# Differential-attention scores: each half on 64 rows of the matmul array, three paired 64-row products, instead of two 128-row products per half

## The chip, the core and the metric

The kernel runs on one core of a Trainium2 chip. The metric is the device time of one execution in microseconds. TensorE (PE in the profile, with its weight loads as PEld) does the matrix products, VectorE (DVE), ScalarE (ACT) and GpSimd (POOL) the elementwise work, and SyncE (SP) issues nearly all DMA transfers.

## The reference

One step of a hybrid attention layer: a normalised input (2048 prompt tokens and 64 sample tokens, 1024 wide) goes through one input projection. Its columns feed eight "fox" heads of forgetting attention (64 wide, causal, with a bias from cumulated log-forget gates) and four heads of differential attention. Outputs are gated, concatenated, projected, normalised and added to the input. The part that the change touches is the differential attention:

```python
def diff_attention(q1, q2, k1, k2, v, lam, rel_bias, q_pos, k_pos):
    ...
        def probs(qi, ki):
            s = jnp.einsum('bqhd,bkhd->bhqk', qi, ki).astype(jnp.float32) * scale + bias
            return jax.nn.softmax(jnp.where(mask, s, NEG_INF), axis=-1)

        p = probs(q1i, k1) - lam * probs(q2i, k2)
        return jnp.einsum('bhqk,bkhd->bqhd', p.astype(v.dtype), v)
```

A differential head has two halves, (q1, k1) and (q2, k2), each 64 wide, that share the values and the bias. The prompt has 2048 queries and keys; the sample has 64 queries on 512 cached and 64 new keys.

## The kernel before

**Precision.** Every float32 operand is split into two float32r parts, h (the rounded value) and l (the rest), and a product is made as h·h + h·l + l·h in float32r.

**Work.** The tokens are cut into four blocks of 512. A unit is two fox heads (units 0 to 3) or one differential head (units 4 to 7). The projection of block b+1 runs beside the attention of block b (class `Proj`, `Attn`), and the output projection beside the last block's attention (class `Out`). Within attention a sub-job is one unit (or one fox head) and one pair of 128-query tiles. Its scores (stage A) run beside the products with the values (stage B) of the sub-job before. The order of the differential units: they come last in blocks 0 and 2, and first in blocks 1 and 3 (line 1424), so that there are two long stretches of differential work.

**Scores before.** `scores()` (L317 to L380) handles one query tile of one half. A head's operand tiles hold 128 rows: 64 rows of the h part and 64 rows of the l part. There are two query tiles for each half, (h|l) and (l|h), and one key tile (h|l). The first product gives h·h + l·l and the second l·h + h·l, so that a chunk of keys (128 to 512 wide, one PSUM bank) costs two products of 128 rows:

```python
                    S = ps.tile([P, BLK], F32, name="S", tag="S", bufs=3)
                    for s in (0, 1):
                        nc.tensor.matmul(S[:rows, :c1 - c0], q()[s][:, qc:qc + rows], kg()[ki][:, c0 - k0:c1 - k0],
                                         start=(s == 0), stop=(s == 1))
```

DVE then adds the bias to each chunk and keeps a running minimum (L359), and ACT takes the exponential (L372). `diff()` (L558) calls `scores()` once for each half and query tile (L578 to L581), then combines both halves (L583). Fox heads use the same `scores()`.

**The values.** `products()` (L463) transposes the probabilities on PE into a PSUM bank named pt (L490), splits them with ACT (L496) and DVE (L497), and multiplies them with the values (L521: av for fox, avd for differential heads).

**PSUM.** There are eight banks: three with the tag S, three with the tag pt, one av and one acc. The projection of the first two blocks borrows S banks (`acc()`, L785).

**What sets the order.** Python lists the work on a line of places (`put`, `merge`), and the tile framework's scheduler then orders the instructions of every engine from its own estimate of their durations. The products of one accumulation may therefore stand apart from one another in PE's stream, with other work between them. PE executes its stream in that order.

**Loads.** Keys and queries pass through DRAM. `k_out()` (L951) stores keys to KS with two DMAs, one for each half; `qgroup()` (L1018) does so for the queries to QD. `want_k()` (L189) loads key tiles into a ring of four slots. `want_q()` (L260) loads the two query tiles of a half with three DMAs into a ring of six slots (L267, L270). `want_kc()` (L200) makes the sample's keys from the cache.

## Time and profile before

| what | us |
|---|---|
| three timed runs | 1841.33, 1835.74, 1825.93 |
| their median | 1835.74 |
| span of the profiled execution, first to last instruction | 1837.8 |
| PE busy in it | 1736.8 |
| DVE busy | 1189.6 |
| ACT busy | 1128.9 |
| POOL busy | 768.2 |

The profiled execution is known by its span; what lies outside its first and last instruction is not shown, and the span stands 2.1 us above the median of the timed runs. A PE matmul row is named by rows*columns of the stationary operand, so that 128*64 means 128 rows and 64 columns of the array in use, and by the moving operand: 128x512 is 128 rows of 512 columns. The duration of a matmul covers its way through the array, and the next matmul begins before it ends; how long PE is held by one is read from the distance of two starts. "x2" merges neighbouring rows of one line.

### The profile page before, as it was taken

To read this page: it belongs to the slowest core of one execution; us is meant where nothing else is said; L and a number is where in the kernel's file an instruction comes from. 1 tells how busy PE (TensorE), PEld (TensorE's weight loads), DVE (VectorE), ACT (ScalarE), POOL (GpSimd) and SP (SyncE) were. 2 spreads that over 40 slices of the span, in tenths; PEclk is the share of its full clock that TensorE was granted. 3 is DMA by queue.
4 is the path that set the end of the run, shared out by engine and by line. 5 is a ranking of instruction groups with operands and counts; after the bars stand their busy time and mean duration, and the time that the engine had idled before them with its cause. 6 is when DMAs were issued, how large, how long until landed. Compare 5 with 4: busy or idle time off the path is not lost. (4 is left out here: it accounts for less than half of the span.)

```text
span 1837.8 us, 31858 instructions
## 1 busy us (share of the span) xinstructions
PE 1736.8 (95%) x9828; PEld 1467.4 (80%) x9828; DVE 1189.6 (65%) x3274; ACT 1128.9 (61%) x2518; POOL 768.2 (42%) x1083
## 2 busy tenths in 40 slices
PE   7888999999999999989999999999989999999998
PEld 5676888777877778878888888888878878887887
DVE  5422555556668576656776678878867876666764
ACT  4533656465767666665666657667776666556663
POOL 2204235345354453343323225555795663322331
PEclk9998999999999999999999999999989999999999
DMA  7787579789868766867777667667665464455433
GB/s 203 240 193 193 162 217 273 205 245 233 218 209 246 213 196 195 233 170 230 219 229 224 177 181 216 195 195 224 199 219 166 145 189 156 153 181 156 145 115 108
DMA packets 308170, 361.38 MB, mean 197 GB/s; under 512 B 41808, under 2 KB 202732, under 8 KB 308000
## 3 DMA queue, kind: packets, MB, share of 16 engines
q1 hardware_dynamic: 306384, 356.93, 66.9%
q0 software_dynamic: 672, 2.38, 0.4%
q8 instruction: 79, 1.29, 0.3%
q14 instruction: 91, 0.75, 0.1%
q10 hardware_dynamic: 944, 0.03, 0.0%
HBM read 263.89 MB, written 97.70 MB: 197 GB/s over the span
## 5 line engine op out<-in xcount | busy, mean ns | idle before, releaser
L372 ACT ACTIVATE prob<-prob,mn 128x1024 f32<-128x1024 f32 (+8 forms) x400 | 356.1, 892 | 180.7 <-DVE mn L359 179.5
L351 PE MATMUL S<-kg,qg 128*128 128x512 f32 (+4 forms) x1344 | 375.8, 373 | 20.5 <-DVE mn L359 10.0
L497 DVE TENSOR_TENSOR ptl<-pt,pth 128x512 fp32r<-128x512 f32 (+3 forms) x456 | 284.4, 636 | 94.8 <-ACT pth L496 92.3
L868 PE MATMUL acc<-wh,xx 128*128 128x512 f32 x752 | 303.4, 408 | 18.9 <-ACT wh L776 14.9
L869 PE MATMUL acc<-wl,xx 128*128 128x512 f32 x752 | 300.6, 401 | 8.5 <-DVE wl L777 8.5
L870 PE MATMUL acc<-wh,xx 128*128 128x512 f32 x752 | 300.6, 400 | 0.1
L496 ACT CAST pth<-pt 128x512 fp32r<-128x512 f32 (+3 forms) x456 | 237.6, 545 | 81.9 <-PE pt L490 65.4
L351 PEld LDWEIGHTS S<-kg,qg 128*128 128x128 f32 (+1 forms) x1344 | 226.6, 188 | 62.0 <-DVE mn L359 18.8
L490 PE MATMUL pt<-ident,prob 128*128 128x128 f32 (+2 forms) x1692 | 257.6, 274 | 4.7 <-ACT pts L637 2.2
L490 PEld LDWEIGHTS pt<-ident,prob 128*128 128x128 f32 (+2 forms) x1692 | 200.2, 142 | 26.6 <-ACT pts L637 3.3
L777 POOL TENSOR_TENSOR wl<-wraw,wh 128x512 fp32r<-128x512 f32 x126 | 167.4, 1345 | 121.2 <-ACT wh L776 91.0
L408 POOL TENSOR_TENSOR dg<-bias,cmask 128x128 f32<-128x128 f32 (+1 forms) x136 | 66.1, 486 | 281.8 <-DVE mn L359 188.4
L868 PEld LDWEIGHTS acc<-wh,xx 128*128 128x128 f32 x752 | 144.2, 193 | 49.7 <-ACT wh L776 17.2
L869 PEld LDWEIGHTS acc<-wl,xx 128*128 128x128 f32 x752 | 144.6, 192 | 37.3 <-DVE wl L777 11.5
L521 PE MATMUL av<-pth,vg 128*128 128x256 f32 (+1 forms) x576 | 158.3, 294 | 9.4 <-DVE oT L537 4.7
L870 PEld LDWEIGHTS acc<-wh,xx 128*128 128x128 f32 x752 | 144.0, 191 | 28.4 <-DVE xx L745 0.6
L521 PE MATMUL av<-ptl,vg 128*64 128x256 f32 (+1 forms) x576 | 140.3, 283 | 3.9 <-DVE ptl L497 3.6
L776 ACT CAST wh<-wraw 128x512 fp32r<-128x512 f32 x168 | 100.5, 618 | 69.1 <-DMA wraw<-in_w_in 59.9
L359 DVE CUSTOM_DVE_ANT_0 prob<-S,bias,mn 128x512 f32<-128x512 f32 (+4 forms) x200 | 115.3, 577 | 28.8 <-DMA bias<-CUM 14.5
L521 PE MATMUL avd<-pth,vg 128*128 128x256 f32 (+1 forms) x576 | 131.6, 288 | 2.3 <-ACT pth L496 2.3
L521 PEld LDWEIGHTS av<-pth,vg 128*128 128x128 f32 x576 | 110.0, 191 | 21.5 <-issue 7.7
L453 POOL TENSOR_SCALAR gate<-gate,rr 128x64 f32<-128x64 f32 (+1 forms) x136 | 61.5, 463 | 140.2 <-DMA gate<-GS 57.9
(257 smaller groups left out, 3611.8 us busy)
## 6 DMA issues: line engine op xcount, KB each, us to landing
wraw<-in_w_in SPq DMA_DIRECT2D x168, 256.0 KB, 4.8
vg<-VS SPq DMA_DIRECT2D x80, 512.0 KB, 4.1
kg<-KS SPq DMA_DIRECT2D x160, 256.0 KB, 4.1
bias<-CUM SPq DMA_DIRECT2D x80, 256.0 KB, 5.6
wst<-in_w_in SPq DMA_DIRECT2D x64, 256.0 KB, 5.6
out<-ef SPq DMA_DIRECT2D x64, 256.0 KB, 3.3
VS<-vhl SPq DMA_DIRECT2D x32, 512.0 KB, 4.6
KS<-khl SPq DMA_DIRECT2D x64, 256.0 KB, 4.7
```

The source lines that it names most:

```text
L351: nc.tensor.matmul(S[:rows, :c1 - c0], q()[s][:, qc:qc + rows], kg()[ki][:, c0 - k0:c1 - k0], start=(s == 0), stop=(s == 1))
L359: nc.vector.tensor_tensor_reduce(out=pr[:rows, a - p0:b - p0], in0=S[:rows, a - c0:b - c0], in1=ap()[:rows, a - b0:b - b0], scale=1.0, sca ...
L372: nc.scalar.activation(out=pr, in_=pr, func=AF.Exp, scale=-1.0, bias=st["m"][:rows, i - 1:i], accum_out=st["s"][:rows, h:h + 1])
L490: nc.tensor.transpose(pt[:rk, off:off + rows], self.key_tile(sts[j], rows, kt, rk), ident[:rows, :rows])
L496: nc.scalar.copy(h[:rk, :off], pt[:rk, :off])
L497: nc.vector.tensor_tensor(out=l[:rk, :off], in0=pt[:rk, :off], in1=r32(h[:rk, :off]), op=ALU.subtract)
L521: nc.tensor.matmul(st["av"][:vs.stop - vs.start, j0 * rows:W], ctxu["v"][kt // 4][:rk, kt % 4, vs], g["p"][part][:rk, o:o + w], start=(kt ...
L776: nc.scalar.copy(h, raw[:, :BLK])
L777: (nc.vector if many or k % 4 == 3 else nc.gpsimd).tensor_tensor(out=l, in0=raw[:, :BLK], in1=r32(h), op=ALU.subtract)
L868: nc.tensor.matmul(a, x[0][:, c0:c0 + rows], wh, start=s, stop=False)
L869: nc.tensor.matmul(a, x[0][:, c0:c0 + rows], wl, start=False, stop=False)
L870: nc.tensor.matmul(a, x[1][:, c0:c0 + rows], wh, start=False, stop=e)
```

## The change

`diff()` now calls a new function, `scores2()`, once for each query tile, for both halves. The operand tiles are laid out anew: one tile holds the h part and one the l part, and in each, rows 0 to 63 belong to the first half and rows 64 to 127 to the second. A chunk of keys takes two S banks, one for each half, and six products of 64 rows: h·h, h·l and l·h, written for the first half on rows 0 to 63 and for the second on rows 64 to 127 in turn. Fox heads keep `scores()`. There are four S banks and two pt banks (three and three before). Stores, loads and the sample's cached keys follow the layout; queries take two loads for a pair of query tiles and both halves (six before), and both halves' key tiles are asked for together. Comments are removed as well, so that line numbers differ.

```diff
+        def want_k2(self, got, u, nk):
+            def load(s, k0, k1):
+                def go():
+                    t = self.p["k"].tile([P, 2 * BLK], F32R, name="kg", tag="k")
+                    for c in range(k0, k1, BLK):
+                        nc.sync.dma_start(out=r32(t[:, c - k0:c - k0 + BLK]), in_=KS[c // BLK][s, u])
+                    got[s].append(t)
+                return go
+            for e in self.key_edges(nk):
+                for s in (0, 1):
+                    self.want(self.K, load(s, *e))
...
-                if s == 0:
+                    if u >= 4:
+                        nc.sync.dma_start(out=r32(t[:, :w]), in_=src[s, u, :, c0:c0 + w])
+                    elif s == 0:
...
-                    S = ps.tile([P, BLK], F32, name="S", tag="S", bufs=3)
+                    S = ps.tile([P, BLK], F32, name="S", tag="S", bufs=4)
...
+        def scores2(self, q, qc, rows, kg, n, bias, sts, last, nk):
...
+            for ki, k0, c0, c1, end in cuts:
+                def chunk(ki=ki, k0=k0, c0=c0, c1=c1, end=end):
+                    S = [ps.tile([P, BLK], F32, name="S", tag="S", bufs=4) for _ in (0, 1)]
+                    for a, b in ((0, 0), (0, 1), (1, 0)):
+                        for i in (0, 1):
+                            r = slice(64 * i, 64 * i + 64)
+                            nc.tensor.matmul(S[i][:rows, :c1 - c0], q()[a][r, qc:qc + rows],
+                                             kg()[b][ki][r, c0 - k0:c1 - k0], start=(a + b == 0), stop=(a == 1))
+                    for half, st in enumerate(sts):
+                        for b0, b1, ap in bias:
...
+                    if last and end:
+                        self.K.free()
+                        self.K.free()
+                th.append(((c1 - c0) * 3 / 2400.0, chunk))
...
-                    pt = ps.tile([P, BLK], F32, name="pt", tag="pt", bufs=3)
+                    pt = ps.tile([P, BLK], F32, name="pt", tag="pt", bufs=2)
...
-                for i in (0, 1):
-                    q = ctxu["q"][(pair, i)]
-                    A += self.scores(lambda q=q: q, j * rows, rows, lambda i=i: ctxu["k"][i], n, pieces, sts[j][i],
-                                     last and j == len(tiles) - 1, ctxu["nk"], i)
+                A += self.scores2(lambda: ctxu["q"][(pair, 0)], j * rows, rows, lambda: ctxu["k"], n, pieces, sts[j],
+                                  last and j == len(tiles) - 1, ctxu["nk"])
...
-                        w = [ask_k(0), ask_k(1), ask_b(0), ask_v] if i == 0 else []
-                        out.append((w + [ask_q(p, 0), ask_q(p, 1), ask_g(p)], A, B, C))
+                        w = [ask_k(0), ask_b(0), ask_v] if i == 0 else []
+                        out.append((w + [ask_q(p, 0), ask_g(p)], A, B, C))
...
+                if g == "dk":
+                    nc.sync.dma_start(out=sc[i, u0:u0 + 4, :, r0:r0 + rows].rearrange("u r t -> r u t"),
+                                      in_=r32(hl[:, i::2, :rows]))
+                    continue
...
+                            if g == "dq":
+                                nc.sync.dma_start(out=QD[b][j, u0 + c, :, i * N:(i + 1) * N],
+                                                  in_=r32(hl[:, j * N:(j + 1) * N]))
+                                continue
```

The scheduler orders the changed program anew. Two places in PE's order show what became of the six products. Both lie in unit 7 of block 2, the last differential unit of that block. S_ is a score bank, kg_ a key tile, qg_ a query tile, pth_ and ptl_ the two parts of transposed probabilities, vg_ the values, avd_ their product, acc_ a projection.

The first place is the second of the four query tiles. Before, around the score chunks S_15746 (first half, 256 keys) and S_15774 (second half, 512 keys):

```order
L521 MATMUL avd_15592<-pth_15650,vg_15112 128x256
L351 MATMUL S_15746<-kg_15429,qg_15231 128x256
L351 MATMUL S_15746<-kg_15429,qg_15233 128x256
L521 MATMUL avd_15592<-pth_15650,vg_15112 128x256
L521 MATMUL avd_15592<-ptl_15651,vg_15112 128x256
L521 MATMUL avd_15592<-pth_15650,vg_15112 128x256
L959 MATMUL ptk_15760<-ident_67,ef_15757 128x128 x4
L870 MATMUL acc_15955<-wh_15524,xx_12042 128x512
L868 MATMUL acc_15955<-wh_15582,xx_12069 128x512
L351 MATMUL S_15774<-kg_15458,qg_15539 128x512
L351 MATMUL S_15774<-kg_15458,qg_15541 128x512
L869 MATMUL acc_15955<-wl_15583,xx_12069 128x512
```

Now, at the first chunk of the same tile, S_15749 for the first half (rows 0 to 63) and S_15750 for the second (rows 64 to 127):

```order
L439 MATMUL S_15749<-kg_15438,qg_14966 128x512
L439 MATMUL S_15749<-kg_15440,qg_14966 128x512
L439 MATMUL S_15749<-kg_15438,qg_14968 128x512
L613 MATMUL avd_15314<-ptl_15471,vg_15205 128x128
L613 MATMUL avd_15314<-pth_15470,vg_15205 128x128
L613 MATMUL avd_15314<-ptl_15471,vg_15205 128x256
L613 MATMUL avd_15314<-pth_15470,vg_15205 128x256 x2
L439 MATMUL S_15750<-kg_15438,qg_14966 128x512
L439 MATMUL S_15750<-kg_15440,qg_14966 128x512
L439 MATMUL S_15750<-kg_15438,qg_14968 128x512
L723 MATMUL pts_15599<-ident_67,oTd_15593 128x128 x2
```

The three products of one half stand together, and 128-row products with the values stand between them and the three of the other half.

The second place is the third query tile of the same unit. Before, two of its chunks for the first half, S_15884 and S_15903:

```order
L351 MATMUL S_15884<-kg_15429,qg_15544 128x512
L521 MATMUL avd_15592<-pth_15783,vg_15181 128x128
L351 MATMUL S_15884<-kg_15429,qg_15546 128x512
L870 MATMUL acc_16139<-wh_15507,xx_12019 128x512
L868 MATMUL acc_16139<-wh_15524,xx_12042 128x512
L351 MATMUL S_15903<-kg_15429,qg_15544 128x384
L351 MATMUL S_15903<-kg_15429,qg_15546 128x384
```

Now, with S_15940 and S_15976 for the first half, S_15941 and S_15977 for the second:

```order
L439 MATMUL S_15940<-kg_15529,qg_15260 128x512
L439 MATMUL S_15941<-kg_15529,qg_15260 128x512
L439 MATMUL S_15940<-kg_15532,qg_15260 128x512
L439 MATMUL S_15941<-kg_15532,qg_15260 128x512
L439 MATMUL S_15940<-kg_15529,qg_15262 128x512
L439 MATMUL S_15941<-kg_15529,qg_15262 128x512
...
L439 MATMUL S_15976<-kg_15529,qg_15260 128x384
L439 MATMUL S_15976<-kg_15532,qg_15260 128x384
L439 MATMUL S_15976<-kg_15529,qg_15262 128x384
L439 MATMUL S_15977<-kg_15529,qg_15260 128x384
L439 MATMUL S_15977<-kg_15532,qg_15260 128x384
L439 MATMUL S_15977<-kg_15529,qg_15262 128x384
```

Before, each chunk is two products, and the first chunk's two stand apart. Now, in the first chunk, the halves alternate, as the code writes them; in the second, three products of one half are followed by three of the other.

Over the whole program the changed order has 1008 products of 64 rows for the differential scores (672 products of 128 rows before). They stand in 231 stretches without other PE work between; 23 stretches are a plain alternation of six, 101 are three products of one half alone (48 of the first, 53 of the second), and 38 are three of one half and then three of the other. The rows of the array in use (128, 64 or 32) change 560 times from one product to the next; before they change 96 times, for small transpositions and the sample.

More of the change, by code (lines that the diff above doesn't have):

```diff
@@ L217, in second @@
                 raw, k0, k1 = t
-                pt = ps.tile([P, BLK], F32, name="ptc", tag="pt", bufs=3)
+                pt = ps.tile([P, BLK], F32, name="ptc", tag="pt", bufs=2)
                 for j in range(4):
                     nc.tensor.transpose(pt[:, j * P:(j + 1) * P], raw[:, j * P:(j + 1) * P], ident)
-                for k, a, b in ((k0, 0, 64), (k1, 64, 0)):
+                if u >= 4:
+                    nc.scalar.copy(k0[:, :PAST], pt)
+                    nc.vector.tensor_tensor(out=k1[:, :PAST], in0=pt, in1=r32(k0[:, :PAST]), op=ALU.subtract)
+                for k, a, b in ((k0, 0, 64), (k1, 64, 0)) if u < 4 else ():
                     nc.scalar.copy(k[a:a + 64, :PAST], pt[a:a + 64])
@@ L539, in gated @@
         def gated(self, gt, oT, u, pair, rows, nt):
-            pt = ps.tile([P, BLK], F32, name="ptg", tag="pt", bufs=3)
+            pt = ps.tile([P, BLK], F32, name="ptg", tag="pt", bufs=2)
             if pair is None:
@@ L604, in endA @@
             def endA():
-                for _ in range(4):
+                for _ in range(2):
                     self.Q.free()
@@ L628, in fin1 @@
             def fin1():
-                pt = e["o"] if sample else ps.tile([P, BLK], F32, name="pts", tag="pt", bufs=3)
+                pt = e["o"] if sample else ps.tile([P, BLK], F32, name="pts", tag="pt", bufs=2)
                 ss = sm.tile([P, 4], F32, name="ssq", tag="ssq")
@@ L663, in go @@
                     def go():
-                        if not sample:
+                        if not sample and u >= 4:
+                            self.want_k2(c["k"], u, nk)
+                        elif not sample:
                             self.want_k(c["k"][hd], u, hd, nk)
@@ L793, in acc @@
                 tag = "pt"
-            return ps.tile([P, BLK], F32, name="acc", tag=tag, bufs=3 if tag in ("S", "pt") else 1)
+            return ps.tile([P, BLK], F32, name="acc", tag=tag, bufs={"S": 4, "pt": 2}.get(tag, 1))
         def block(self, b):
@@ L889, in go @@
                         a.append(ps.tile([P, BLK], F32, name="acc", tag="av", bufs=1))
-                        a.extend(ps.tile([P, BLK], F32, name="accS", tag="S", bufs=3) for _ in range(3))
+                        a.extend(ps.tile([P, BLK], F32, name="accS", tag="S", bufs=4) for _ in range(3))
                     for i, t in enumerate(tl):
@@ L1067, in col @@
             def col():
-                pt = ps.tile([P, BLK], F32, name="ptq", tag="pt", bufs=3)
+                pt = ps.tile([P, BLK], F32, name="ptq", tag="pt", bufs=2)
                 for i in range(5):
@@ L1158, in sample @@
                 nc.sync.dma_start(out=lf_s, in_=z[:DEC, 32:40])
-                pt = ps.tile([P, BLK], F32, name="pts", tag="pt", bufs=3)
+                pt = ps.tile([P, BLK], F32, name="pts", tag="pt", bufs=2)
                 nc.tensor.transpose(pt[:8, :DEC], z[:DEC, 32:40], ident[:DEC, :DEC])
@@ L1264, in go @@
                         tag = ("acc", "S", "S", "S", "pt", "pt", "pt", "av")[2 * (t - 12) + n] if late else "acc"
-                        e["acc"][n] = ps.tile([P, BLK], F32, name="acco", tag=tag, bufs=3 if tag in ("S", "pt") else 1)
+                        e["acc"][n] = ps.tile([P, BLK], F32, name="acco", tag=tag, bufs={"S": 4, "pt": 2}.get(tag, 1))
                     wh, wl = self.w[k][0][n][:, :BLK], self.w[k][1][n][:, :BLK]
```

59 lines of the change are left out of this document (55 added, 4 removed).

## The prediction

> **What bounds the kernel now.** I read the page first.
>
> ```profile
> span 1837.8 us, 31858 instructions
> PE 1736.8 (95%) x9828; PEld 1467.4 (80%) x9828; DVE 1189.6 (65%) x3274; ACT 1128.9 (61%) x2518; POOL 768.2 (42%) x1083
> ```
>
> PE is busy for 95% of the span and no other engine comes near. The change acts only where differential units run, so I cut out the two stretches that hold them, with one row for each: us of the stretch, then busy time of each engine.
>
> ```profile
> 340.00:650.00 310.00, 290.50 (x1546) 236.41 (x1546) 200.44 (x543) 201.44 (x514) 138.76 (x230) 0.98 0.81 226
> 1000.00:1505.00 505.00, 489.05 (x2809) 417.57 (x2808) 388.11 (x1029) 340.70 (x751) 282.25 (x318) 0.99 0.65 192
> ```
>
> PE is busy 290.5 of 310 us and 489.1 of 505 us there. It idles 19.5 + 16.0 = 35.5 us, while DVE, the next engine, idles for 227 us of the 815. The granted clock is 0.98 and 0.99, so throttling plays no part. PE sets the pace in both stretches: a microsecond more on PE's stream is a microsecond more of span, except for what falls into those 35.5 us.
>
> **What the scores cost now.** The groups of score products, each shape apart:
>
> ```profile
> L351 PE MATMUL S<-kg,qg 128*128 128x512 f32 x800 | 259.3, 410 | 6.1 <-DVE mn L359 5.7 <-DVE fz L1139 0.2
> L351 PE MATMUL S<-kg,qg 128*128 128x384 f32 x224 | 63.2, 355 | 10.9 <-DMA qg<-QD 5.3 <-DVE mn L359 2.9 <-DVE ptl L497 2.5
> L351 PE MATMUL S<-kg,qg 128*128 128x256 f32 x224 | 49.2, 295 | 2.5 <-DVE mn L359 1.3 <-issue 1.1
> L351 PE MATMUL S<-kg,qg 128*128 128x128 f32 x32 | 5.8, 252 | 0.5 <-DMA qg<-QD 0.5
> L351 PE MATMUL S<-kg,qg 128*64 128x288 f32 x64 | 13.3, 304 | 0.5 <-ACT ef L878 0.5
> ```
>
> Half of each group belongs to the differential units: 400, 112, 112, 16 and 32 products. The 410 ns of the mean is the way through the array, not what a product holds PE for. That is the distance of starts, and a timeline of PE shows it. This window also holds the most telling thing in the trace, one 64-row instruction among 128-row ones:
>
> ```profile
> 529.67 0.42 PE L351 MATMUL S<-kg,qg 128*64 128x288 f32 x2
> 529.93 0.28 PE L521 MATMUL avd<-pth,vg 128*128 128x256 f32 x1
> 530.14 0.27 PE L544 MATMUL ptg<-ident,gate 64*128 64x64 f32 x1
> 530.35 0.50 PE L868 MATMUL acc<-wh,xx 128*128 128x512 f32 x1
> 530.68 0.39 PE L869 MATMUL acc<-wl,xx 128*128 128x512 f32 x1
> 530.91 0.39 PE L870 MATMUL acc<-wh,xx 128*128 128x512 f32 x1
> 531.14 0.40 PE L868 MATMUL acc<-wh,xx 128*128 128x512 f32 x1
> ```
>
> A 512-column product holds PE for 0.23 us (530.68 to 530.91 to 531.14) and the 288-column products 0.13 (0.26 for two). Another two windows give 256 and 384 columns:
>
> ```profile
> 1336.72 0.51 PE L351 MATMUL S<-kg,qg 128*128 128x384 f32 x2
> 1337.07 0.38 PE L633 MATMUL pts<-ident,oTd 128*128 128x128 f32 x2
> 1337.28 0.27 PE L490 MATMUL pt<-ident,prob 128*128 128x128 f32 x1
> ```
> ```profile
> 1565.21 0.28 PE L521 MATMUL av<-ptl,vg 128*64 128x256 f32 x1
> 1565.33 0.28 PE L521 MATMUL av<-pth,vg 128*128 128x256 f32 x1
> 1565.45 0.28 PE L521 MATMUL av<-ptl,vg 128*64 128x256 f32 x1
> 1565.56 0.38 PE L490 MATMUL pt<-ident,prob 128*128 128x128 f32 x2
> ```
>
> 384 columns hold PE for 0.175 us (0.35 for two), 256 columns for 0.12, and I put 128 at half of that, 0.06. So the differential scores hold PE for 400 x 0.23 + 112 x 0.175 + 112 x 0.12 + 16 x 0.06 + 32 x 0.13 = 130 us.
>
> **The change, first term: the products themselves.** Now there are 1008 products on half of the array's rows: 600, 168, 168, 24 and 48 of the same widths. If two of them on different halves of the rows share the array whenever they follow each other, a pair counts once. Were all paired, it would be half of 195, 98 us: 32.6 us less than now. But the changed order does not keep the pairs. Only 23 stretches alternate as written; in 101 three products of one half stand alone, and in 38 three follow three, so that only the two in the middle meet. Counting neighbours on different halves as one over the whole order leaves 214 pairs (118, 35, 28, 9, 24 of the five widths) and 580 singles (381, 94, 99, 6, 0): 499 x 0.23 + 129 x 0.175 + 127 x 0.12 + 15 x 0.06 + 24 x 0.13 = 157 us. That is **26 us more** than now. The trace of before has no two tiles side by side on the rows, so the overlap itself is unknown: with none it is 195 us, 65 more. I take 26, since the two halves share neither rows, weights nor banks, and keep both ends.
>
> **Second term: going in and out of 64 rows.** Look again at the window above. The 256-column avd should hold PE for 0.12 us, but the 64-row transposition starts 0.21 after it. The 64-column transposition should take about 0.06 (two 128-column transpositions of 0.27 each take 0.38 at 1565.56, so one holds PE for 0.11), but the next 128-row product starts 0.21 later, and that one's follower 0.33 later instead of 0.23. Together 0.75 us pass where 0.12 + 0.06 + 0.23 = 0.41 would do: the visit costs 0.34 us. PE's weight loads in the same window show why:
>
> ```profile
> 529.80 0.19 PEld L521 LDWEIGHTS avd<-pth,vg 128*128 128x128 f32 x1
> 530.14 0.14 PEld L544 LDWEIGHTS ptg<-ident,gate 64*128 64x128 f32 x1
> 530.34 0.19 PEld L868 LDWEIGHTS acc<-wh,xx 128*128 128x128 f32 x1
> 530.45 0.19 PEld L869 LDWEIGHTS acc<-wl,xx 128*128 128x128 f32 x1
> 530.68 0.19 PEld L870 LDWEIGHTS acc<-wh,xx 128*128 128x128 f32 x1
> ```
>
> Normally a load starts with the start of the product before it and is hidden (529.80 for the product at 529.93, 530.68 for the one at 530.91). At the change of rows it starts only at 530.14 and 530.34, with its own product: PE empties first, and then the load is exposed. A second visit has the same distances:
>
> ```profile
> 715.50 0.28 PE L521 MATMUL av<-ptl,vg 128*64 128x256 f32 x1
> 715.71 0.27 PE L544 MATMUL ptg<-ident,gate 64*128 64x64 f32 x1
> 715.91 0.62 PE L351 MATMUL S<-kg,qg 128*128 128x384 f32 x2
> ```
>
> Changing the columns costs nothing of the kind: at 1565.21 to 1565.56 the stream goes from 128*64 to 128*128 and back at 0.12 us each. The Trainium skill says, in "TensorEngine Tiling (Array Packing)", section Tiling Modes, that changing the tiling mode, not just the tile, drains TensorE. For rows the trace agrees (0.21 against 0.12); for columns it does not, and taken for both the rule would give no other sum here, because the column changes are as many before as now.
>
> A score stretch opens with a 0.19 us load of float32r weights (530.34) rather than 0.14 (530.14), so a visit costs 0.34 + 0.05 = 0.39. The order changes its rows 560 times instead of 96: 464 more, 232 visits. 232 x 0.39 = **90 us**. Bounds: if only the two waits before the loads remain (0.09 each), 0.18 a visit, 42 us; if the second half's first load, 0.11 (530.34 to 530.45), cannot lie beside the first, 0.50, 116 us.
>
> **Third term: what the idle time takes.** The extra PE work stretches intervals in which DVE, ACT and the queues catch up, so part of the 35.5 us of idle goes. Transitions between blocks remain. I take **15 us** off; the bounds are 0 and 35.
>
> **Fourth term: banks and loads.** Transpositions have two banks instead of three. A bank is held from the transposition through ACT's and DVE's pass:
>
> ```profile
> L497 DVE TENSOR_TENSOR ptl<-pt,pth 128x512 fp32r<-128x512 f32 (+3 forms) x456 | 284.4, 636 | 94.8 <-ACT pth L496 92.3
> L496 ACT CAST pth<-pt 128x512 fp32r<-128x512 f32 (+3 forms) x456 | 237.6, 545 | 81.9 <-PE pt L490 65.4 <-PE av L521 13.9 <-DVE ptl L497 0.3
> L351 PE MATMUL S<-kg,qg x1344: 218/389/793, 200.2 to 1777.0; 128*128 128x512 f32 x119, 128*128 128x256 f32 x30, 128*128 128x384 f32 x29, 128*64 128x288 f32 x9
> ```
>
> That is 0.545 + 0.636 = 1.2 us, so two banks let a group through every 0.6 us, while 456 groups in the 1577 us from the first score product to the last are one every 3.5. The cover is the projection and score work between them; where it is gone, at the head of a sub-job with its two transpositions ahead, a wait of one DVE pass (0.64) in each of the 96 prompt sub-jobs would be 60 us. On the other side four score banks and fewer query loads can remove waits:
>
> ```profile
> PE S L351 <- DVE mn L359: 10.0, 13, 2.7
> PE S L351 <- DMA qg<-QD: 5.8, 6, 2.5
> ```
>
> Both together are 16 us at most, against a first chunk that now needs both halves' keys. I take **+5**, near the lower end because the order was laid out for two banks; the bounds are -16 and +60. DVE and ACT pass over the same score chunks as before, so they add nothing; the queue loses 144 query loads, which PE does not wait for beyond the 5.8.
>
> **Sum.** 1837.8 + 26 + 90 - 15 + 5 = 1944 against this execution's span, which is 2.1 us above the median of the runs: **1942 us**, 5.8% slower.
>
> **The rivals.**
> *No sharing of the array.* Products on different halves run one after the other. No row of this trace speaks for or against it; that the halves have rows, weights and banks of their own speaks against it. The first term is then 65: 1981 us. Chance 0.12.
> *Cheap visits.* A stretch of score products often begins after a wait, or the loads for 64 rows go in while the array empties: 42 instead of 90, 1894 us. For it speaks that the quoted visits have a transposition inside, whose mode may carry part of the cost; against it, that the wait stands on the 128-row side too, in front of ordinary projection weights. Chance 0.11.
> *Row changes are as free as column changes* in this form: float32r in, two PSUM banks out. The place is the 232 visits, the price 0. Then 26 us of products meet 35.5 us of idle and the time is 1837.8 + 26 - 35.5 - 2.1 = 1826 us: not slower, within 1%. It decides once a visit costs less than (35.5 - 26) / 232 = 0.04 us. Both quoted visits show eight times that. Chance 0.04.
> *All pairs share.* The order's separated halves overlap none the less, with free visits: 32.6 us less, 1803 us, and faster. The order of PE speaks against it, with 128-row products between the halves. The same page of the Trainium skill gives up to twofold for a contraction of at most 64 rows (Overview); nothing here shows it. Chance 0.03.
>
> **How the numbers follow.** My forecast has 0.70; with its visits at 0.34 to 0.45, its idle time and banks at their nearer ends, it covers about 1915 to 1970. The range must reach to the cases with 0.12 and 0.11, so 1890 to 1985. A measurement of this kernel can tell about 1% from no change. Slower by over 1% are the forecast and the first two rivals, 0.93; within 1% the third, 0.04; faster the last, 0.03.
>
> **What would show it.** In the profile after: the span of the two stretches grows by about 100 us and the others' hardly; around each score stretch the starts are 0.21 apart where 0.12 is due, and the first load of a stretch starts with its product; in the alternating stretches two products start within one 0.23 us, and alone standing threes at 0.23 each. PE stays the busiest engine, and DVE's share falls. I am wrong if the rows change without a late load, if six alternating products take six times 0.23, or if PE waits for DVE ptl (L497 of before) in front of transpositions for tens of microseconds.

## The result: 7.8% slower, and where the time went

| | before | after |
|---|---|---|
| median of the timed runs, us | 1837.83 (4 runs) | 1976.62 (4 runs) |
| lowest and highest | 1825.93 and 1841.33 | 1969.98 and 1979.61 |
| span of the profiled execution | 1837.8 | 1975.0 |

The ratio is 1.078, with a 95% interval from 1.073 to 1.083. Of the runs behind the tables here and below, one of the changed kernel with the banks of before was a slow one of 9949 us, and the ratios leave it out. The time lies inside the predicted range, 35 us above the predicted 1942. That closeness hides errors in three of the four terms, and the largest is in the one that the prediction thought almost nothing of. The page after begins:

```profile
span 1975.0 us, 32108 instructions
...
PE 1853.1 (94%) x10164; PEld 1476.4 (75%) x10164; DVE 1168.1 (59%) x3270; ACT 1134.0 (57%) x2514; POOL 766.9 (39%) x1083
```

PE is still the engine that sets the pace, with 116 us more busy time. But it also idles more: 1975.0 - 1853.1 = 121.9 us, against 101.0 before. The prediction expected its idle time to shrink.

**Not only the differential stretches grew.** The next two answers cut both executions where the products with the values change from fox heads to differential heads and back. Each row has the stretch, its length, then busy time (and instructions) of PE, PEld, DVE, ACT and POOL, the granted clock, and DMA. The rows are, in turn, differential, fox, differential, fox. Before:

```profile
373.20:667.10 293.90, 277.52 (x1500) 226.99 (x1499) 196.47 (x524) 198.36 (x501) 142.11 (x238) 0.99 0.79 224
667.10:1123.10 456.00, 439.96 (x2618) 373.92 (x2617) 309.37 (x936) 289.12 (x617) 161.23 (x231) 0.99 0.73 209
1123.10:1539.20 416.10, 399.49 (x2282) 342.49 (x2280) 321.99 (x831) 283.03 (x637) 259.35 (x293) 0.98 0.64 192
1539.20:1806.50 267.30, 257.05 (x1591) 223.17 (x1589) 179.27 (x509) 160.65 (x329) 83.09 (x132) 0.99 0.46 141
```

After:

```profile
368.60:684.80 316.20, 302.62 (x1611) 225.69 (x1609) 180.64 (x516) 198.51 (x497) 142.58 (x241) 1.00 0.66 201
684.80:1181.60 496.80, 467.94 (x2664) 384.52 (x2664) 310.46 (x936) 296.42 (x624) 162.69 (x229) 0.97 0.63 187
1181.60:1648.60 467.00, 449.19 (x2405) 336.30 (x2402) 302.91 (x819) 272.20 (x609) 247.15 (x276) 0.96 0.50 156
1648.60:1941.70 293.10, 266.25 (x1591) 225.84 (x1592) 185.21 (x515) 163.73 (x337) 87.07 (x141) 0.98 0.42 131
```

The differential stretches grew by 22 and 51 us. The fox stretches, whose score products are the same as before, grew by 41 and 26. In the last one PE executes the same 1591 products, and its idle time goes from 10.2 to 26.9 us. Something that fox heads share with differential heads has become dearer. The waits of PE after (what it waited for, us in total, times, longest) name it:

```profile
PE av L613 <- ACT pth L588: 19.5, 13, 4.2
...
PE S L370 <- DVE mn L378: 11.5, 11, 4.0
PE pt L582 <- DVE ptl L589: 9.1, 15, 1.8
...
PE avd L613 <- ACT pth L588: 6.1, 2, 4.5
```

The two passes that wait on either side have their durations of before (0.638 and 0.544 us, against 0.636 and 0.545), but ACT now idles 216.4 us for transpositions, 65.4 before:

```profile
L589 DVE TENSOR_TENSOR ptl<-pt,pth 128x512 fp32r<-128x512 f32 (+3 forms) x456 | 287.1, 638 | 159.1 <-ACT pth L588 156.3
L588 ACT CAST pth<-pt 128x512 fp32r<-128x512 f32 (+3 forms) x456 | 243.7, 544 | 221.0 <-PE pt L582 216.4
```

**The visits are as predicted.** This window of PE after shows three products of one half alone (start, us, operation):

```profile
526.29 0.39 PE L962 MATMUL acc<-wh,xx 128*128 128x512 f32 x1
526.51 0.39 PE L960 MATMUL acc<-wh,xx 128*128 128x512 f32 x1
526.83 0.96 PE L439 MATMUL S<-kg,qg 64*128 64x512 f32 x3
527.72 0.50 PE L961 MATMUL acc<-wl,xx 128*128 128x512 f32 x1
528.06 0.40 PE L962 MATMUL acc<-wh,xx 128*128 128x512 f32 x1
```

The product at 526.51 is followed after 0.32 us instead of 0.23. The three take 0.89 (526.83 to 527.72) instead of 0.69. The first product behind them is followed after 0.34. The extra 0.09 + 0.20 + 0.11 = 0.40 us is the price of a visit. The weight loads show the late first load that was looked for; the first starts with its product, not with the one before:

```profile
526.29 0.19 PEld L960 LDWEIGHTS acc<-wh,xx 128*128 128x128 f32 x1
526.83 0.52 PEld L439 LDWEIGHTS S<-kg,qg 64*128 64x128 f32 x3 [0.35 <-DVE ptl L589]
527.72 0.19 PEld L961 LDWEIGHTS acc<-wl,xx 128*128 128x128 f32 x1 [0.37 <-issue]
```

Over the visits that no recorded wait interrupts, the medians of the same three distances are 0.093, 0.202 and 0.107 us beyond the products' own time: 0.40 again.

**The halves share the array, and more often than the order promises.** Two more stretches of the same timeline:

```profile
351.36 0.79 PE L439 MATMUL S<-kg,qg 64*128 64x384 f32 x6
352.07 0.50 PE L960 MATMUL acc<-wh,xx 128*128 128x512 f32 x1
```
```profile
575.37 0.97 PE L439 MATMUL S<-kg,qg 64*128 64x512 f32 x6
576.27 0.50 PE L962 MATMUL acc<-wh,xx 128*128 128x512 f32 x1
```

The first is an alternation as the code writes it: six products of 384 columns in 0.71 us, that is three times 0.175 and the 0.20 of the visit. In the second the order has three of one half and then three of the other:

```order
L439 MATMUL S_6905<-kg_6118,qg_6369 128x512
L439 MATMUL S_6905<-kg_6121,qg_6369 128x512
L439 MATMUL S_6905<-kg_6118,qg_6371 128x512
L439 MATMUL S_6906<-kg_6118,qg_6369 128x512
L439 MATMUL S_6906<-kg_6121,qg_6369 128x512
L439 MATMUL S_6906<-kg_6118,qg_6371 128x512
L962 MATMUL acc_7014<-wh_6191,xx_6902 128x512
```

They take 0.90 us, as long as the three that stood alone (0.89). Their starts come in three couples, 10 to 16 ns apart, with 0.34, 0.23 and 0.33 us from one couple to the next and to the product behind. All three of the second half ran beside the three of the first, though they stand behind them in the stream. So PE does not start every product in the order of its stream, as the text on the kernel before has it. The prediction let only the two in the middle meet.

### The profile page after: what moved, and what is told of

It reads as the page before. It is cut to its first block, busy times and chain, and to the rows that moved or that the text cites. A ratio compares the mean times of both kernels' runs of the same rounds, so it can differ in the third digit from the quotient of the medians.

```text
span 1975.0 us, 32108 instructions
## 1 busy us (share of the span) xinstructions
PE 1853.1 (94%) x10164; PEld 1476.4 (75%) x10164; DVE 1168.1 (59%) x3270; ACT 1134.0 (57%) x2514; POOL 766.9 (39%) x1083
## 4 chain that ended last, share of the span: by engine, by line
PE 61%; DMA 13%; DVE 6%; ACT 6%; issue 3%; POOL 3%; SPq 1%; DVEq 0%; ACTq 0%; POOLq 0%
PE S L439 7%; PE pt L582 7%; PE acc L960 6%; PE acc L961 6%; PE acc L962 6%; PE av L613 4%; PE avd L613 4%; DMA wraw<-in_w_in 4%; PE S L370 4%; PE acco L1374 3%; PE acco L1376 2%; PE acco L1375 2%; PE acc L1099 2%; PE acc L1097 2%; PE acc L1098 2%
## 5 line engine op out<-in xcount | busy, mean ns | idle before, releaser
L588 ACT CAST pth<-pt 128x512 fp32r<-128x512 f32 (+3 forms) x456 | 243.7, 544 | 221.0 <-PE pt L582 216.4
L960 PE MATMUL acc<-wh,xx 128*128 128x512 f32 x752 | 305.7, 410 | 17.3 <-ACT wh L868 12.8
L582 PE MATMUL pt<-ident,prob 128*128 128x128 f32 (+2 forms) x1692 | 267.9, 280 | 12.5 <-DVE ptl L589 9.1
L391 ACT ACTIVATE prob<-prob,mn 128x1024 f32<-128x1024 f32 (+5 forms) x200 | 177.9, 891 | 63.5 <-DVE mn L378 63.1
L439 PE MATMUL S<-kg,qg 64*128 64x512 f32 (+4 forms) x1008 | 206.7, 394 | 3.7 <-DVE mn L448 2.5
L464 ACT ACTIVATE prob<-prob,mn 128x1024 f32<-128x1024 f32 (+6 forms) x200 | 177.5, 890 | 52.9 <-DVE mn L448 52.4
L370 PE MATMUL S<-kg,qg 128*128 128x512 f32 (+4 forms) x672 | 184.8, 374 | 14.1 <-DVE mn L378 11.5
L613 PE MATMUL av<-pth,vg 128*128 128x256 f32 (+1 forms) x576 | 159.5, 291 | 19.5 <-ACT pth L588 19.5
L439 PEld LDWEIGHTS S<-kg,qg 64*128 64x128 f32 (+1 forms) x1008 | 113.0, 185 | 64.0 <-issue 28.8
L613 PE MATMUL av<-ptl,vg 128*64 128x256 f32 (+1 forms) x576 | 154.5, 304 | 0.6 <-DVE ptl L589 0.4
L370 PEld LDWEIGHTS S<-kg,qg 128*128 128x128 f32 (+1 forms) x672 | 110.0, 188 | 34.1 <-DVE mn L378 20.3
```

Source lines behind the costliest of these rows:

```text
L391: nc.scalar.activation(out=pr, in_=pr, func=AF.Exp, scale=-1.0, bias=st["m"][:rows, i - 1:i], accum_out=st["s"][:rows, h:h + 1])
L439: nc.tensor.matmul(S[i][:rows, :c1 - c0], q()[a][r, qc:qc + rows], kg()[b][ki][r, c0 - k0:c1 - k0], start=(a + b == 0), stop=(a == 1))
L464: nc.scalar.activation(out=pr, in_=pr, func=AF.Exp, scale=-1.0, bias=st["m"][:rows, i - 1:i], accum_out=st["s"][:rows, h:h + 1])
L582: nc.tensor.transpose(pt[:rk, off:off + rows], self.key_tile(sts[j], rows, kt, rk), ident[:rows, :rows])
L588: nc.scalar.copy(h[:rk, :off], pt[:rk, :off])
L613: nc.tensor.matmul(st["av"][:vs.stop - vs.start, j0 * rows:W], ctxu["v"][kt // 4][:rk, kt % 4, vs], g["p"][part][:rk, o:o + w], start=(kt ...
```

## The experiments

Each run had a theory A and a rival, which its expectation states. Ratios are to the kernel before, run on the same chip.

| kernel | S and pt banks | median us | ratio, 95% interval |
|---|---|---|---|
| after | 4, 2 | 1976.62 | 1.078 (1.073 to 1.083) |
| before with the banks of after | 4, 2 | 1922.83 | 1.049 (1.045 to 1.052) |
| after with the banks of before | 3, 3 | 1919.09 | 1.046 (1.042 to 1.051) |
| before, visits alone | 3, 3 | 1890.41 | 1.031 (1.028 to 1.034) |
| after, pairs kept, banks of before | 3, 3 | 1927.61 | 1.051 (1.048 to 1.054) |
| after, full rows | 4, 2 | 1953.13 | 1.065 (1.062 to 1.068) |
| after, pairs kept | 4, 2 | 1959.63 | 1.069 (1.066 to 1.072) |
| before, four transposition banks | 2, 4 | 1918.98 | 1.046 (1.042 to 1.050) |
| before, two transposition banks | 3, 2 | 1934.05 | 1.055 (1.053 to 1.057) |
| after, banks freed early | 4, 2 | 1957.10 | 1.066 (1.061 to 1.071) |
| before, banks freed early | 3, 3 | 1865.21 | 1.016 (1.012 to 1.020) |
| after, 3 and 3 banks, freed early | 3, 3 | 1910.90 | 1.040 (1.035 to 1.044) |
| before, 4 and 2 banks, freed early | 4, 2 | 1919.09 | 1.045 (1.043 to 1.048) |

### The banks alone

The kernel before, with nothing changed but the numbers of banks:

```diff
-                    S = ps.tile([P, BLK], F32, name="S", tag="S", bufs=3)
+                    S = ps.tile([P, BLK], F32, name="S", tag="S", bufs=4)
...
-                    pt = ps.tile([P, BLK], F32, name="pt", tag="pt", bufs=3)
+                    pt = ps.tile([P, BLK], F32, name="pt", tag="pt", bufs=2)
```

> The kernel before with one thing of the change: four score banks and two transposition banks instead of three and three. The scores stay products of 128 rows. Theory A (the two transposition banks cause the growth of the fox stretches, which was 46 + 26 = 72 us): about 1838 + 72 = 1910 us, with PE waiting for ACT and DVE at the transpositions and the products with the values. Theory B (the fox stretches grew because the changed scores shifted the order of everything else, not because of the banks): within 10 us of before, about 1840 us.

Measured: 1922.83 against 1835.19, 88 us more without one 64-row product. The waits of PE in this kernel:

```profile
PE S L351 <- DVE mn L359: 19.2, 18, 3.7
PE pt L490 <- DVE ptl L497: 17.3, 26, 3.0
...
PE av L521 <- ACT pth L496: 13.5, 11, 3.1
```

Before, the three were 10.0, 0.5 and 2.2 us. That is theory A's side, with more than its 72. So the term that the prediction put at 5 us is worth 88 by itself, beyond its upper bound of 60. It is not the fox stretches alone that pay: cut as above, they grow by 37 and 15 us here, and the differential stretches by 25 and 9.

### The change with the banks of before

The opposite edit, in the changed kernel: `bufs=3` for both tags.

> The changed kernel with three score banks and three transposition banks, as before the change. Its order has 29 more visits to 64 rows (619 changes of the rows) and 65 fewer pairs, worth 29 x 0.39 = 11 us and 12 us on PE. Theory A (two transposition banks cost the 72 us): 1977 - 72 + 23 = about 1928 us. Theory B (they cost nothing): 1977 + 23 = 2000 us.

Measured: 1919.09, 84 us above the kernel before and 57 below the change. PE's two groups in this kernel (busy, mean ns, then idle time before them and its causes):

```profile
L582 PE MATMUL pt<-ident,prob 128*128 128x128 f32 (+2 forms) x1692 | 257.9, 274 | 3.4 <-ACT pts L727 1.3 <-DVE mix L646 0.9 <-DVE ptl L589 0.7
L439 PE MATMUL S<-kg,qg 64*128 64x512 f32 (+4 forms) x1008 | 226.2, 393 | 1.2 <-DVE mn L448 0.7 <-DMA kg<-KS 0.3
```

The transpositions' wait for DVE is 0.7 us again (9.1 in the change), and the two fox stretches take 455.5 and 261.8 us from their first to their last product (443.5 and 267.3 before, 489.5 and 293.1 in the change). That is theory A's side. The fourth score bank would account for most of the difference between 57 and 88: with four, 286 couples of products share the array in the trace and 231 visits are made, with three 201 and 265. That is 15 us of products and 14 of visits on the array, and 57 + 29 = 86. How much of the 29 reaches the time was not measured.

### The visits alone

The kernel before, whose differential score products use rows 0 to 63 only:

```diff
-                        nc.tensor.matmul(S[:rows, :c1 - c0], q()[s][:, qc:qc + rows], kg()[ki][:, c0 - k0:c1 - k0],
+                        nc.tensor.matmul(S[:rows, :c1 - c0], q()[s][:R, qc:qc + rows], kg()[ki][:R, c0 - k0:c1 - k0],
```

> The kernel before, with its differential score products cut to rows 0 to 63 of both operands: as many products as before (672), no pairs, three and three banks, and only the visits to 64 rows added (655 changes of the rows instead of 96, 280 visits). It leaves out the part of every differential score that lies on rows 64 to 127. Theory A (a visit holds PE for 0.39 us, and 35 to 42 us of it fall into idle time): 1838 + 109 - 40 = about 1907 us. Rival (visits are cheap, 0.18 us, because they begin after waits): 1838 + 50 - 35 = about 1853 us.

Measured: 1890.41, 55 us more. In the trace there are 288 visits, and the medians of the three distances are 0.093, 0.200 and 0.106 us, 0.40 together as in the change. That is 115 us on PE's stream, of which 60 do not appear in the time. PE's idle time shrinks by 34 us, from 101.0 to 1892.6 - 1825.2 = 67.4. So a visit costs what was predicted, and the kernel absorbs far more than the 15 us allowed for. Neither number expected was met: the time lies between them.

### Every pair kept, with the banks of before

The changed kernel with three and three banks, and each product of a chunk but the first pinned behind the one before it in the order:

```diff
-                        for i in (0, 1):
+                        for i in (1, 0):
...
+                            if (a, b, i) != (0, 0, 1):
+                                tc.keep_in_program_order(m)
```

> The changed kernel with three and three banks, and with each product of a chunk pinned behind the one traced before it, so that the halves alternate: 438 pairs and 132 singles (149 and 710 with three and three banks unpinned), 539 changes of the rows. Theory A (two products on different halves share the array, a visit costs 0.39 us): the products hold PE for 111 us, 18 less than before, 222 visits cost 87: 1838 - 18 + 87 - 40 of idle = about 1867 us. Rival (no sharing): products 194 us, 1838 + 65 + 87 - 40 = about 1950 us.

Measured: 1927.61, no gain over 1919.09. The trace has 415 couples that share instead of 201 and 239 visits instead of 265, which saves some 42 and 10 us on the array. (The visits stay many because the first product of a chunk, which nothing pins, stands alone 61 times in the order.) The waits of the same run say where that went:

```profile
L370 PE MATMUL S<-kg,qg 128*128 128x512 f32 (+4 forms) x672 | 186.9, 377 | 15.8 <-DVE mn L378 15.0 <-DVE rr L524 0.3 <-DVE kg L241 0.3
L439 PE MATMUL S<-kg,qg 64*128 64x512 f32 (+4 forms) x1008 | 186.7, 410 | 11.0 <-DVE mn L450 9.5 <-DVE ssum L471 0.8 <-DMA kg<-KS 0.5
```

With three score banks the differential scores' wait for DVE rises from 0.7 to 9.5 us and that of the fox scores from 4.1 to 15.0. Sharing the array needs two of the three banks at one moment, and PE then waits until DVE has emptied them. In all PE idles 1922.4 - 1810.5 = 111.9 us, 40 more than with three banks and no pinning, and the time at half of the clock that follows such waits (below) costs 39 us instead of 15. Together these 40 and 24 us are 12 more than the 52 that were saved; the spans differ by 14. Neither time that was expected is met.

### Full rows, with the banks of the change

The changed kernel, its products on all 128 rows, so that there are neither visits nor sharing (its sums run over both halves):

```diff
-                            r = slice(64 * i, 64 * i + 64)
+                            r = slice(0, P)
```

> The changed kernel (four and two banks) with its six products a chunk on all 128 rows: no product on 64 rows, so no visits and no sharing. The score that it computes is the sum over both halves' rows for either half, so the differential outputs are not the reference's. Theory A (in the changed kernel a visit holds PE for 0.40 us, and of what PE gains or loses in the differential stretches about half reaches the span; the two transposition banks cost about 85 by themselves): 1835 + 85 + 65/2 for three products where there were two = about 1950 us, 25 below the changed kernel although its products hold PE for 39 us more. Rival (visits are hidden behind waits and only the product time counts): 1977 + 39 = about 2015 us.

Measured: 1953.13, as theory A had it. Six full products with no sharing are 23 us quicker than six half ones that share: the visits cost more than the sharing saves. Of its 120 us above the kernel before, 65 are products (195 instead of 130) and 88 the banks; some 33 are absorbed.

### Every pair kept, with the banks of the change

The pinning, with four and two banks.

> The changed kernel, four and two banks, with each product of a chunk pinned behind the one traced before it: 431 pairs and 146 singles (214 and 580 unpinned), 584 changes of the rows (560). Products hold PE for 112 us instead of 156, twelve more visits cost 5. Theory A (pairs share; half of PE's gain reaches the span): 1977 - 39/2 = about 1957 us, between 1938 and 1970. Rival (keeping the pairs makes both halves wait for two banks at once, and this takes the gain as it did with three banks): 1977 us or more.

Measured: 1959.63, 17 us less than the change, close to the 1957 expected. Here 419 couples share, 115 us of products by the prediction's own durations, against 143 in the change. With a fourth score bank most of these 28 us are kept, where with three nothing was.

### Which of the two bank counts it is

Two kernels split the edit of the banks: four transposition banks with two score banks, and two transposition banks with three score banks (one PSUM bank stays empty).

> The kernel before with two score banks and four transposition banks. Theory A (PE's stream suffers where a transposition waits for a bank, and three are already enough for most groups): the gain of a fourth is small, up to 10 us, and two score banks cost at least as much: 1835 to 1870 us. Rival (transposition banks are what the kernel lacks): 1800 to 1825 us.

Measured: 1918.98, 86 us more. Both expectations fail: neither saw that the scores need their third bank as much. PE's wait in front of the scores is 31.0 us now, 10.0 before:

```profile
PE S L351 <- DVE mn L359: 31.0, 41, 5.0
```

> The kernel before with three score banks and two transposition banks, one bank of the eight unused. Theory A (the loss of the third transposition bank makes the 87 us of four and two banks): 1835 + 87 = about 1922 us, at least 1910. Rival (the fourth score bank, through another order of the scores, makes a part of it): 1835 to 1890 us.

Measured: 1934.05, 101 us more, as theory A had it. Taking one transposition bank away costs 101 us, and giving that bank to the scores brings back some 11 to 14. In the kernel before, three and three is a balance from which a step to either side costs about 85 us.

### Is it the time that a bank is held?

If a bank is held through ACT's and DVE's passes (0.54 + 0.64 us), freeing it after ACT's should make two banks nearly as good as three. DVE's pass was made to read the h part from SBUF instead of the bank; it then takes 0.784 us in the mean instead of 0.638, and the l part becomes zero:

```diff
-                    nc.vector.tensor_tensor(out=l[:rk, :off], in0=pt[:rk, :off], in1=r32(h[:rk, :off]),
+                    nc.vector.tensor_tensor(out=l[:rk, :off], in0=r32(h[:rk, :off]), in1=r32(h[:rk, :off]),
```

The edit does more than free the bank. In the change so edited, 257 of the 336 passes over 512 columns take 0.69 us as without it, but 79, each begun while a POOL instruction ran, take longer, up to 2.6 us, and POOL's busy time rises from 767 to 829 us.

> The changed kernel (four S, two transposition banks) in which DVE's pass that makes the l part of the transposed probabilities reads the h part from SBUF instead of the transposition bank. It leaves out the l part of the probabilities (it becomes zero); every instruction stays, but a transposition bank is held only through ACT's pass of 0.54 us instead of ACT's and DVE's 1.18. Theory A, that the change pays for the third transposition bank because the groups come in bursts and each holds a bank through two passes: with half the holding time two banks do what three did, so the time falls from 1977 to about 1920 (1905 to 1935), the time of the changed kernel with three and three banks; PE's waits for DVE ptl in front of transpositions go from 9.1 us to under 3, and the half-clock stretches after 215 us from 15 to under 8. Rival B, that the holding time does not matter and the time comes from the changed order of the instructions or from the four S banks: within 1% of 1977.

> The kernel before (three and three banks) with the same edit: the l part of the transposed probabilities is left out (zero), every instruction stays, and a transposition bank is free after ACT's pass. Theory A: with three banks PE waited only 0.5 us for DVE ptl in front of transpositions, so there is little to win: 1815 to 1840. Rival B, that a shorter hold makes any version quicker, whatever its banks: as much as in the changed kernel, 40 us or more, so below 1795.

Measured: 1957.10 and 1865.21. Theory A misses both; rival B misses the second, and the first stands at the very edge of its 1%. The signs of theory A fail too: 13 half-clock stretches after 215 us instead of under 8, and at the transpositions PE waits 6.7 us for ACT where it waited 9.1 for DVE. The edit costs the kernel before 31 us, and the change gains 20 in spite of it. Two more kernels complete the square:

> The changed kernel with three S and three transposition banks, and DVE's pass reading the h part from SBUF (the l part of the transposed probabilities is left out, zero; every instruction stays). That edit lengthens DVE's pass from 0.64 to 0.78 us and by itself costs the kernel before 31 us (1865 against 1834); in the changed kernel with two transposition banks it gained 20 (1957). Theory A, that the price of the third bank is the holding time: under the short hold three banks are worth little over two, so this is 1919 + 31 = 1950, and stands less than 25 us under 1957. Rival B, that the 57 us between three and two banks come from the order or the fourth S bank, whatever the hold: 1957 - 57 = 1900.

> The kernel before with four S and two transposition banks and the same edit (the l part of the transposed probabilities is left out, zero; every instruction stays). Without the edit the banks cost 87 us (1923 against 1835). Theory A: under the short hold they cost at most 30, so between 1865 and 1895. Rival B, that the banks cost the same whatever the hold: 1865 + 87 = 1952.

Measured: 1910.90 and 1919.09.

| | 3 and 3 banks | 4 and 2 banks | price of the banks |
|---|---|---|---|
| before | 1835 | 1923 | 88 |
| before, freed early | 1865 | 1919 | 54 |
| changed products | 1919 | 1977 | 57 |
| changed products, freed early | 1911 | 1957 | 46 |

The price falls by 34 and 11 us, far less than theory A wanted. The 34 speaks against rival B; the 11 is no more than the scatter of the runs (1903 to 1916 us in the third kernel). What was wrong is the holding time itself. Following each of the 456 groups through the trace, from its first transposition to the end of the last pass that reads the bank, gives these means:

| mean time that a transposition bank is held, us | 3 and 3 | 4 and 2 |
|---|---|---|
| before | 4.19 | 3.18 |
| before, freed early | 3.69 | 2.47 |
| changed products | 4.09 | 3.07 |
| changed products, freed early | 3.67 | 2.35 |

It is three to four us without the edit, not 1.2, and freeing the bank before DVE's pass shortens it by no more than a quarter. Nor is it a constant: with one bank less it is a us shorter. The trace of before shows why. These are PE, ACT and DVE around one place:

```profile
878.45 0.60 PE L490 MATMUL pt<-ident,prob 128*128 128x128 f32 x4
...
879.18 1.03 PE L490 MATMUL pt<-ident,prob 128*128 128x128 f32 x8
```
```profile
879.14 0.59 ACT L496 CAST pth<-pt 128x512 fp32r<-128x512 f32 x1 [0.48 <-PE pt L490]
...
880.14 1.15 ACT L372 ACTIVATE prob<-prob,mn 128x1024 f32<-128x1024 f32 x1
...
881.29 0.60 ACT L372 ACTIVATE prob<-prob,mn 128x384 f32<-128x384 f32 x1
...
881.89 1.05 ACT L496 CAST pth<-pt 128x512 fp32r<-128x512 f32 x2
```
```profile
880.48 0.69 DVE L497 TENSOR_TENSOR ptl<-pt,pth 128x512 fp32r<-128x512 f32 x1
...
882.48 1.29 DVE L497 TENSOR_TENSOR ptl<-pt,pth 128x512 fp32r<-128x512 f32 x2
```

Twelve transpositions, three groups, fill all three banks between 878.45 and 880.0. The first is free at 881.17 (880.48 + 0.69). The other two wait while ACT works through two exponentials that stand ahead in its queue; ACT comes to them at 881.89, DVE at 882.48, and the second bank is free at about 883.2, four us after its first transposition. With two banks and the same order the third group could not have been transposed before 881.17, and PE's stream would have stood behind it.

What stays open is how the rest divides between PE standing in front of a bank and the scheduler's other order for fewer banks, since each of these kernels is ordered anew. In the last kernel PE still waits for the banks, now for ACT, which holds them to the end:

```profile
PE pt L490 <- ACT pth L496: 14.9, 16, 2.4
```

### Half of the clock after a wait

Waits are dearer than they look. PE after, around a wait in a fox stretch, with the granted clock (the number after POOL's) below:

```profile
727.40 0.38 PE L613 MATMUL av<-pth,vg 128*128 128x256 f32 x1 [0.37 <-ACT pth L588]
731.82 1.35 PE L370 MATMUL S<-kg,qg 128*64 128x288 f32 x4 [4.04 <-DVE mn L378]
...
734.22 0.42 PE L613 MATMUL av<-pth,vg 128*128 128x256 f32 x1
734.44 0.41 PE L613 MATMUL av<-ptl,vg 128*64 128x256 f32 x1
734.65 0.31 PE L613 MATMUL av<-pth,vg 128*128 128x128 f32 x1
```
```profile
727.50:729.00 1.50, 0.28 (x1) 0.08 (x1) 0.00 (x0) 0.74 (x2) 0.72 (x2) 1.00 1.04 349
729.00:731.50 2.50, 0.00 (x0) 0.00 (x0) 0.30 (x1) 0.00 (x0) 0.00 (x0) 0.52 0.62 169
731.50:735.50 4.00, 3.68 (x15) 2.74 (x16) 3.33 (x16) 0.59 (x1) 2.15 (x3) 0.50 0.16 47
735.50:738.00 2.50, 2.50 (x17) 2.12 (x15) 1.95 (x9) 1.95 (x6) 0.33 (x1) 0.91 0.56 181
```

PE stands still for 4.04 us. After 1.3 us of standing still the granted clock drops to half, and it stays there until about 4 us after work has resumed (the 0.91 of the last row is half for its first 0.45 us): 256-column products are 0.22 and 0.21 us apart (734.22, 734.44, 734.65) instead of 0.12. So this wait costs 4 us and then 2 more. Counted over the executions, with half of PE's busy time in such stretches as their cost:

| | half-clock stretches | their cost, us | PE idle, us |
|---|---|---|---|
| before | 14 | 28 | 101.0 |
| before, 4 and 2 banks | 20 | 45 | 145.6 |
| before, 3 and 2 banks | 22 | 48 | 152.5 |
| after, 3 and 3 banks | 7 | 15 | 71.6 |
| after | 18 | 41 | 121.9 |

Of the 83 us by which the banks alone lengthen the span, 45 are idle time and about 17 clock. By the distances of starts, some 15 of the rest stand in front of the recorded waits, whose first part passes while the product before still runs through the array, and some 7 are waits too short to be recorded, for the same reason. The Trainium skill says, in "TensorE: Matmul & The Clock Gate", section Part 1: The HAM clock gate, that the array runs at half clock after an idle window and returns to full after about 3.4 us of work; the trace agrees in the half and roughly in the 4 us. It does not agree in the idle window: of the 3.4 us before the clock fell, PE had stood still for only 1.7 (0.37 before the product at 727.40 and 1.3 behind it).

## Why the prediction was right, and where its terms were wrong

The direction was right, and so was the mechanism that the prediction put first. The sizes of three terms were not. The ledger in us, with the measured term beside the predicted:

| term | predicted | measured | from |
|---|---|---|---|
| products | +26 | +13 | 286 couples and 436 singles in the trace, by the prediction's durations: 143 instead of 130 |
| visits | +90 | +92 | 231 x 0.40 |
| absorbed | -15 | about -55 | visits alone: 115 on PE, 55 in the time; change with 3 and 3 banks: 28 + 106 on PE, 84 in the time |
| banks | +5 | about +88 | banks alone |
| sum | +106 | +138 | the spans' difference: 1975.0 - 1837.8 = 137 |

The measured sum closes better than its terms are known: the absorbed part was 60 us in one of the two kernels and 50 in the other, and the 88 was measured without visits.

**Products.** That the halves share was right: in nearly all couples the two starts lie within 20 ns. The step that failed is that where three products of one half follow three of the other, "only the two in the middle meet". All six pair, in 0.90 us. The rival without sharing gave 1981, the nearest of all to 1977, but its mechanism is refuted; the agreement is chance.

**Visits.** Right in place, in mechanism (the late first load) and in price: 0.40 for 0.39. Cheap visits (0.18) and free ones are refuted by the same distances.

**Absorbed.** The step took some of "the 35.5 us of idle" in the two differential stretches as all there was. It was too narrow twice. With the changed products and three and three banks, PE's idle time falls from 101.0 to 71.6 us, of which 20 fall inside those stretches and the rest outside; and the half-clock stretches fall from 14 to 7, worth 13 us. What takes the remainder was not followed. The prediction read a clock of 0.98 and 0.99 as "throttling plays no part", and missed that the last per cent is the price of waits: 14 half-clock stretches, 28 us.

**Banks.** The step that failed is "0.545 + 0.636 = 1.2 us, so two banks let a group through every 0.6 us, while 456 groups [...] are one every 3.5". Both sides of that comparison were wrong, and both could have been read from the trace of before. A bank is held 4.19 us there, because it waits for its turn on ACT and on DVE. And the mean distance of 3.5 us hides bursts: the median distance between DVE's passes over two groups is 1.99 us. Followed through the trace of before, 125 of the 456 groups begin while two earlier ones still hold their banks, and for 209 us all three banks are held by such groups at once; with two banks those 125 cannot begin where they stand. The cover "between them" is not there when it is needed, and not only "at the head of a sub-job". The fox stretches, with 67 us of the growth, pay for a bank which only the differential heads asked for; with the banks alone they pay 52 us, and the differential stretches 34.

The test that the prediction set itself, "if PE waits for DVE ptl [...] for tens of microseconds", reads 9.1 us in the change and 17.3 with the banks alone. It looked at one wait of several: one level on, PE waits 19.5 us in the change for ACT's pass over the transposed bank. Its forecast that the other stretches "hardly" grow failed outright, and of all its signs this one shows the error best.

No kernel tried beats the one before. The nearest that compute the whole are 4.6% slower.

## What to carry to other kernels

Price a buffer by the time from its first write to its last read as the trace shows it, with the queues that it waits in, and compare that with the distance inside bursts; the sum of the passes over it and the mean rate flatter it. When a change takes a shared resource from one part of a kernel, look for the cost in the parts that it does not touch. By these figures half-row products on TensorE pay only where long stretches of them stand together: a visit costs 0.40 us, nearly two 512-column products, while six that all share save only 0.23 against the four full-row products that they replace.

## What the runs showed of the hardware

- Products on different halves of the rows overtake: three that stand in the stream behind three of the other half start beside them, and six take 0.90 us where three take 0.89. The Trainium skill, "TensorE: Matmul & The Clock Gate", section Part 3: Packing small matmuls, calls matmuls strictly first in, first out; the measured stretch does not agree, as in that order only the third and the fourth could meet.
- A 64-row stretch costs 0.09 us at its entry, 0.20 inside and at its exit, and 0.11 behind it. The median in the change is 0.39 us for 1 product in it, 0.47 for 2, 0.40 for 3 and 0.41 for 6, whether or not they share.
- The granted clock is half from 1.3 us into a wait of 4.04 us until about 4 us after it. In the traces of all fourteen kernels, 214 of 228 half-clock stretches last 3.41 us or a whole multiple of it.
- DVE's subtraction over 512 columns takes 0.69 us with one operand in PSUM, and as long with one SBUF tile for both, unless POOL is in the way. In the change freed early all 79 of the 336 passes that take over 0.75 us began while a POOL instruction ran (71 others began so and did not); with one operand in PSUM none of 336 takes over 0.70, though 150 begin so.
